# Row means of a 512 MiB array: loop loads moved from SyncE's hardware queue to GpSimd's software queue, eight runs as one packet

## The chip, the cores and the metric

The kernel runs on one core of a Trainium2 chip. The metric is the device time of one execution in microseconds (us); lower is better. The core has five engines that work side by side: TensorE (PE), VectorE (DVE), ScalarE (ACT), GpSimd (POOL) and SyncE (SP). They order their work by semaphores. Data moves between the chip's memory (HBM) and the on-chip buffers (SBUF, 128 partitions) through 16 DMA engines, which all issuing engines share.

## The reference

```python
def setup_inputs():
    return {
        "x": np.random.randn(64, 256, 8192).astype(np.float32),
    }

def reference(x: np.ndarray) -> np.ndarray:
    return np.mean(x, axis=2)
```

The input has 64 x 256 = 16384 rows of 8192 float32 numbers, 536.87 MB. The output is the mean of each row, 16384 numbers.

## The kernel before

**Tiling.** Each of the 128 partitions owns 127 consecutive rows. They are taken two at a time: 63 loads (NB) of two rows each, 64 KB for a partition, 8 MiB in all; the text calls them load 0 to load 62. The 127th owned row comes alone ("one", 4 MiB). The last 128 rows of the array are split into quarters, one quarter row for a partition, and come as four groups of 1 MiB, the last of them cut into four pieces, so that little work is left once the last bytes land.

**Buffers.** There are three SBUF buffers of 64 KB for a partition (NBUF = 3). Load g goes into buffer g mod 3. "one" and the groups use buffer 0 again at the end.

**SyncE issues every load** (lines 109 to 131). First come load 0 in two parts (L114 with a quarter of one row, L115 with the rest), load 1 and load 2 (L117). Then a loop of 20 rounds (L118) issues loads 3 to 62: for each of the three buffers it waits until the buffer's free semaphore is at least 1, takes 1 off it (L120), and issues the load (L121), whose address hangs on the loop's counter. Behind the loop SyncE waits for free semaphore 0 again and issues "one" (L125), three groups (L127) and four pieces (L129). At the end it stores the results (L133, L135).

**VectorE adds up.** It goes through the loads in order. A loop of 20 rounds (L160) waits for a buffer's arrival semaphore, which counts 16 for a load, takes the 16 off (L162), and reduces the buffer's two rows to two sums (L163); the end of the reduction adds 1 to the buffer's free semaphore. Loads 60 and 61 are reduced at L173. Load 62, "one", the groups and one piece go through `halves` (L145), one instruction that adds the two halves of its operand and sums up the result; one piece has a reduction of its own (L196).

**The others.** GpSimd prepares a small selection matrix (L81 to L93), waits for the owned rows' sums and multiplies them by 1/8192 (L104); their store leaves at L133. ScalarE sums two pieces (L209). TensorE adds the four quarters of the last rows (L218), and VectorE and ScalarE copy that to the row which is stored at L135.

**Order around the change.** All loads go through one hardware queue in the order of issue. A load of the loop can't be issued before the reduction that frees its buffer has ended. Each DMA engine moves the share of eight partitions, so eight runs of 64 KB of a full load.

The loop of the issuing engine:

```python
with eng.Fori(0, ROUNDS) as i:
    for b in range(NBUF):
        eng.wait_ge(free_sems[b], 1).then_inc(free_sems[b], -1)
        eng.dma_start(bufs[b][:], later[b][:, bass.ds(i, 1), :]).then_inc(
            in_sems[b], 16
        )
```

Of the kernel before, what the change touches and what calls it, by code (L numbers as in the profile page):

```python
# [6 lines left out]
ADD = mybir.AluOpType.add  # L7
X = mybir.AxisListType.X
# [3 lines left out]
def bass_global_avg_pool_1d_kernel(  # L12
# [6 lines left out]
    B, C, L = x.shape  # L19
# [4 lines left out]
    NB = OWN // 2  # L24
    NBUF = 3
    ROUNDS = NB // NBUF - 1
# [12 lines left out]
    owned = flat[0 : P * OWN, :].rearrange("(p r) l -> p (r l)", p=P)  # L39
# [4 lines left out]
    with ExitStack() as ctx:  # L44
        sb = lambda n, s: ctx.enter_context(nc.sbuf_tensor(n, s, F32))
        sem = lambda n: ctx.enter_context(nc.semaphore(n))
        res = sb("res", [P, OWN])
# [5 lines left out]
        bufs = [sb(f"buf{i}", [P, 2 * L]) for i in range(NBUF)]  # L53
# [3 lines left out]

        in_sems = [sem(f"in_sem{i}") for i in range(NBUF)]
        free_sems = [sem(f"free_sem{i}") for i in range(NBUF)]
        first_sem = sem("first_sem")  # L60
        one_sem = sem("one_sem")
        group_sems = [sem(f"group_sem{j}") for j in range(PER - 1)]
        piece_sems = [sem(f"piece_sem{c}") for c in range(NP)]
        owned_sem = sem("owned_sem")
# [9 lines left out]

        one = bufs[0][:, 0:L]
        group = lambda j: bufs[0][:, L + j * W : L + (j + 1) * W]

        eng = nc.gpsimd  # L80
# [18 lines left out]
            pattern=[[PER, G]],  # L99
            channel_multiplier=-1,  # L100
        ).then_inc(sel_sem, 1)
        eng.wait_ge(free_sems[0], 1)
        eng.wait_ge(owned_sem, 4)
        eng.tensor_scalar(  # L104
            scaled[:], res[:], inv, None, op0=mybir.AluOpType.mult
# [2 lines left out]

        eng = nc.sync
        pair = lambda g: owned[:, 2 * g * L : 2 * (g + 1) * L]  # L110
        later = owned[:, 2 * NBUF * L : 2 * NB * L].rearrange(
            "p (i b w) -> b p i w", i=ROUNDS, b=NBUF
        )
        eng.dma_start(bufs[0][:, 0:FIRST], owned[:, 0:FIRST]).then_inc(first_sem, 16)  # L114
        eng.dma_start(bufs[0][:, FIRST:], owned[:, FIRST : 2 * L]).then_inc(in_sems[0], 16)  # L115
        for b in range(1, NBUF):
            eng.dma_start(bufs[b][:], pair(b)).then_inc(in_sems[b], 16)  # L117
        with eng.Fori(0, ROUNDS) as i:  # L118
            for b in range(NBUF):
                eng.wait_ge(free_sems[b], 1).then_inc(free_sems[b], -1)  # L120
                eng.dma_start(bufs[b][:], later[b][:, bass.ds(i, 1), :]).then_inc(  # L121
                    in_sems[b], 16
                )
        eng.wait_ge(free_sems[0], 1)
        eng.dma_start(one, owned[:, 2 * NB * L :]).then_inc(one_sem, 16)  # L125
        for j in range(PER - 1):
            eng.dma_start(group(j), groups[j]).then_inc(group_sems[j], 16)  # L127
# [13 lines left out]
        eng = nc.vector  # L141

        def halves(ap, to, done):
            n = ap.shape[1] // 2
            eng.tensor_tensor_reduce(  # L145
                ap[:, 0:n],
                ap[:, 0:n],
                ap[:, n : 2 * n],
                scale=1.0,
                scalar=0.0,  # L150
                op0=ADD,
                op1=ADD,
                accum_out=to,
            ).then_inc(done, 1)

        eng.wait_ge(first_sem, 16)
        early = res[:, 0 : 2 * ROUNDS * NBUF].rearrange(
            "p (i b j) -> p i b j", i=ROUNDS, b=NBUF
        )
        with eng.Fori(0, ROUNDS) as i:  # L160
            for b in range(NBUF):
                eng.wait_ge(in_sems[b], 16).then_inc(in_sems[b], -16)  # L162
                eng.tensor_reduce(  # L163
                    early[:, bass.ds(i, 1), b, :],
                    bufs[b][:].rearrange("p (j l) -> p j l", j=2),
                    X,
                    ADD,
                ).then_inc(free_sems[b], 1)
        for b in range(NBUF):
            g = NB - NBUF + b  # L170
            eng.wait_ge(in_sems[b], 16)
            if b < 2:
                eng.tensor_reduce(  # L173
                    res[:, 2 * g : 2 * g + 2],
                    bufs[b][:].rearrange("p (j l) -> p j l", j=2),
                    X,
                    ADD,
                ).then_inc(free_sems[0] if b == 0 else owned_sem, 1)
            else:
                for j in range(2):  # L180
                    halves(
                        bufs[b][:, j * L : (j + 1) * L],
                        res[:, 2 * g + j : 2 * g + j + 1],
                        owned_sem,
                    )
# [17 lines left out]
        eng = nc.scalar  # L203
        for n, c in enumerate((0, 2)):
# [3 lines left out]
            to = PER - 1 + c  # L208
# [5 lines left out]
        eng = nc.tensor  # L214
# [45 lines left out]
```

## Time and profile before

| | |
|---|---|
| median of the 3 runs shown | 1243.48 us (1243.43 to 1244.08) |
| profiled execution | 1243.53 us |
| span of its instructions | 1242.3 us |
| VectorE busy | 1085.5 us in 78 instructions |
| HBM read | 536.87 MB, 432 GB/s over the span |
| transfers of the loop (L121) | 60, SyncE busy 333 ns with each issue |
| `halves` on 4096 + 4096 numbers (L145) | 3, mean 4424 ns |

The profile is of one execution. Its span runs from the first to the last instruction of the core; the execution's own time is 1.2 us longer. In a line of a group, the first part names the source line, the engine, the operation and the tiles with their shapes; behind the bar stand the busy time in total, the mean of one in ns, and the time for which the engine was idle just before such instructions, with what ended it. A line of the timeline has the start, the duration, the engine, the line and what it does; in square brackets stands the idle time before. Lines with DMA_DIRECT2D are issues of transfers; the number behind the size, or the last one, is the median time from issue to landing. In the view of slices the span is cut into 40 equal parts of 31 us, and GB/s is what the 16 DMA engines moved in each.

### The profile page before, as it was taken

How to read it: one execution, taken by the hardware profiler on the slowest of the kernel's cores; microseconds unless marked ns; L12 is line 12 of the kernel's file. 1: busy time of each engine (PE TensorE's matmuls, PEld its weight loads, DVE VectorE, ACT ScalarE, POOL GpSimd, SP SyncE). 2: the span in 40 equal slices, each digit the busy share in tenths (PEclk: the TensorE clock that was granted, in tenths of full speed). 3: DMA queues.
4: the chain of work that ended last, by engine and by line, in shares of the span. 5: the costliest groups of instructions: out<-in, count | busy, mean ns of one | idle time of the engine just before them, and what ended most of it. 6: DMA issues, size and time to landing. Idle time of an engine off the chain costs nothing. (4 is left out here: it accounts for less than half of the span.)

```text
span 1242.3 us, 636 instructions
## 1 busy us (share of the span) xinstructions
PE 1.7 (0%) x14; PEld 0.6 (0%) x14; DVE 1085.5 (87%) x78; ACT 3.0 (0%) x6; POOL 2.1 (0%) x8
## 2 busy tenths in 40 slices
PE   0000000000000000000000000000000000000000
PEld 0000000000000000000000000000000000000000
DVE  2898988989889898898898988989889898898988
ACT  0000000000000000000000000000000000000000
POOL 0000000000000000000000000000000000000000
DMA  9999999999999999999999999999999999999998
GB/s 405 439 439 439 439 433 411 439 439 439 439 439 422 422 439 439 439 439 439 433 411 439 439 439 439 439 437 407 439 439 439 439 439 437 409 437 439 439 439 374
DMA packets 10514, 536.94 MB, mean 432 GB/s; under 512 B 1297, under 2 KB 1554, under 8 KB 1810
## 3 DMA queue, kind: packets, MB, share of 16 engines
q1 hardware_dynamic: 10514, 536.94, 99.8%
HBM read 536.87 MB, written 0.07 MB: 432 GB/s over the span
## 5 line engine op out<-in xcount | busy, mean ns | idle before, releaser
L163 DVE TENSOR_REDUCE res<-buf 128x16384 f32 x60 | 1033.2, 17220 | 146.8 <-DVEq L162 146.8
L173 DVE TENSOR_REDUCE res<-buf 128x2 f32<-128x16384 f32 x2 | 34.4, 17220 | 4.0 <-DMA buf<-in_x_dram 4.0
L145 DVE CUSTOM_DVE_ANT_0 buf<-buf 128x4096 f32<-128x4096 f32 (+2 forms) x7 | 17.3, 2497 | 4.1 <-DMA buf<-in_x_dram 4.1
L209 ACT ACTIVATE buf<-buf 128x896 f32<-128x896 f32 (+1 forms) x2 | 1.4, 711 | 1236.7 <-DMA buf<-in_x_dram 1236.6
L104 POOL TENSOR_SCALAR scaled<-res 128x127 f32<-128x127 f32 x1 | 1.4, 1362 | 1233.3 <-DVE res L145 1233.3
L218 PE MATMUL psum<-sel,part 128*1 128x32 f32 x14 | 1.7, 225 | 1239.2 <-DVE part L145 1238.3
L209 ACT ACT_TABLE_LOAD x1 | 1.3, 1283 | 0.8 <-PEq L245 0.8
L218 PEld LDWEIGHTS psum<-sel,part 128*1 128x1 f32 x14 | 0.6, 81 | 1240.1 <-issue 1235.9
L196 DVE TENSOR_REDUCE part<-buf 128x1 f32<-128x256 f32 x1 | 0.4, 420 | 0.4 <-DMA buf<-in_x_dram 0.4
L200 DVE COPY row<-psum 1x32 f32<-1x32 f32 x1 | 0.2, 179 | 0.4 <-PE psum L218 0.4
L209 ACT ACTIVATION_READ_ACCUMULATOR buf<-buf 128x1 f32 x2 | 0.4, 188 | 0.0
L145 DVE DVE_READ_ACCUMULATOR2_ANT part<- 128x1 f32 x4 | 0.3, 82 | 0.0
L145 DVE DVE_READ_ACCUMULATOR2_ANT res<- 128x1 f32 x3 | 0.2, 83 | 0.0
L211 ACT ACTIVATE row<-psum 1x96 f32<-1x96 f32 x1 | 0.2, 223 | 0.0
L93 POOL TENSOR_SCALAR_AFFINE_SELECT sel<-sel 128x32 f32<-128x32 f32 x1 | 0.2, 215 | 0.1
L83 POOL TENSOR_SCALAR_AFFINE_SELECT sel<-sel 128x32 f32<-128x32 f32 x1 | 0.2, 213 | 0.1
L81 POOL MEMSET sel<- 128x32 f32 x1 | 0.1, 125 | 0.3 <-POOLq L245 0.3
L245 POOL MEMSET const-uint8-127<- 128x1 uint8 x1 | 0.1, 103 | 0.0
L245 POOL MEMSET const-bfloat16-1.0<- 128x1 bf16 x1 | 0.1, 102 | 0.0
L245 POOL MEMSET const-float32-0.0<- 128x1 f32 x1 | 0.1, 99 | 0.3 <-issue 0.3
L245 POOL MEMSET const-float32-1.0<- 128x1 f32 x1 | 0.1, 99 | 0.0
## 6 DMA issues: line engine op xcount, KB each, us to landing
buf<-in_x_dram SPq DMA_DIRECT2D x1, 7168.0 KB, 21.1
buf<-in_x_dram SPq DMA_DIRECT2D x4, 1024.0 KB, 34.1
buf<-in_x_dram SPq DMA_DIRECT2D x1, 4096.0 KB, 31.1
buf<-in_x_dram SPq DMA_DIRECT2D x62, 40.3
buf<-in_x_dram SPq DMA_DIRECT2D x1, 448.0 KB, 37.7
buf<-in_x_dram SPq DMA_DIRECT2D x1, 288.0 KB, 37.9
buf<-in_x_dram SPq DMA_DIRECT2D x1, 160.0 KB, 37.9
buf<-in_x_dram SPq DMA_DIRECT2D x1, 128.0 KB, 37.8
```

Of the source, the lines that this page charges most:

```text
L83: eng.affine_select(out=sel[:], in_=sel[:], compare_op=mybir.AluOpType.is_ge, fill=0.0, base=0, pattern=[[-PER, G]], channel_multiplier=1, ...
L93: eng.affine_select(out=sel[:], in_=sel[:], compare_op=mybir.AluOpType.is_ge, fill=0.0, base=PER - 1, pattern=[[PER, G]], channel_multipli ...
L104: eng.tensor_scalar(scaled[:], res[:], inv, None, op0=mybir.AluOpType.mult).then_inc(pool_sem, 1)
L145: eng.tensor_tensor_reduce(ap[:, 0:n], ap[:, 0:n], ap[:, n : 2 * n], scale=1.0, scalar=0.0, op0=ADD, op1=ADD, accum_out=to,).then_inc(done, 1)
L163: eng.tensor_reduce(early[:, bass.ds(i, 1), b, :], bufs[b][:].rearrange("p (j l) -> p j l", j=2), X, ADD,).then_inc(free_sems[b], 1)
L173: eng.tensor_reduce(res[:, 2 * g : 2 * g + 2], bufs[b][:].rearrange("p (j l) -> p j l", j=2), X, ADD,).then_inc(free_sems[0] if b == 0 els ...
L196: eng.tensor_reduce(part[:, PER + 2 : PER + 3], group(PER - 1)[:, a:z], X, ADD).then_inc(part_d, 1)
L200: eng.tensor_copy(row[:, P - G : P], psum[1][:, 0:G]).then_inc(row_sem, 1)
L209: eng.activation(ap, ap, COPY, accum_out=part[:, to : to + 1]).then_inc(part_a, 1)
L211: eng.activation(row[:, 0 : P - G], psum[0][:, 0 : P - G], COPY).then_inc(row_sem, 1)
L218: return eng.matmul(dst, part[:, n : n + 1], sel[:], start=start, stop=stop)
L245: nc = _bacc.Bacc("TRN2", target_bir_lowering=False, num_devices=1)
```

## The change

Loads 0 to 2 and the last loads ("one", groups, pieces) stay with SyncE. Loads 3 to 62 are issued by GpSimd, whose transfers go through a queue of its own with descriptors made by software. The loop has the same 20 rounds of three and the same wait for the free semaphore. Each transfer carries `single_packet=True`: the eight runs of a DMA engine are to make one packet.

The loads of the loop count on semaphores of their own (`soft_sems`), which are no longer counted down: VectorE waits for 16 more in each round, with a value that a register holds. The first three reductions stand ahead of VectorE's loop, which has 19 rounds now. The end of the reduction of load 60 is told by a new semaphore (`last_sem`), for which both SyncE (ahead of "one") and GpSimd (ahead of its scaling, now L116) wait. The shapes and the number of reductions are the same.

```diff
+        soft_sems = [sem(f"soft_sem{i}") for i in range(NBUF)]
+        last_sem = sem("last_sem")
...
         eng = nc.gpsimd
...
-        eng.wait_ge(free_sems[0], 1)
+        later = owned[:, 2 * NBUF * L : 2 * NB * L].rearrange(
+            "p (i b w) -> b p i w", i=ROUNDS, b=NBUF
+        )
+        with eng.Fori(0, ROUNDS) as i:
+            for b in range(NBUF):
+                eng.wait_ge(free_sems[b], 1).then_inc(free_sems[b], -1)
+                eng.dma_start(
+                    bufs[b][:], later[b][:, bass.ds(i, 1), :], single_packet=True
+                ).then_inc(soft_sems[b], 16)
+        eng.wait_ge(last_sem, 1)
         eng.wait_ge(owned_sem, 4)
...
         eng = nc.sync
...
-        with eng.Fori(0, ROUNDS) as i:
-            for b in range(NBUF):
-                eng.wait_ge(free_sems[b], 1).then_inc(free_sems[b], -1)
-                eng.dma_start(bufs[b][:], later[b][:, bass.ds(i, 1), :]).then_inc(
-                    in_sems[b], 16
-                )
-        eng.wait_ge(free_sems[0], 1)
+        eng.wait_ge(last_sem, 1)
         eng.dma_start(one, owned[:, 2 * NB * L :]).then_inc(one_sem, 16)
...
         eng = nc.vector
...
+        def sums(to, b):
+            return eng.tensor_reduce(
+                to, bufs[b][:].rearrange("p (j l) -> p j l", j=2), X, ADD
+            )
+
+        for b in range(NBUF):
+            eng.wait_ge(in_sems[b], 16)
+            sums(res[:, 2 * b : 2 * b + 2], b).then_inc(free_sems[b], 1)
...
-        with eng.Fori(0, ROUNDS) as i:
+        with eng.Fori(0, ROUNDS - 1) as i:
             for b in range(NBUF):
-                eng.wait_ge(in_sems[b], 16).then_inc(in_sems[b], -16)
...
+                eng.wait_ge(soft_sems[b], i * 16 + 16)
+                sums(early[:, bass.ds(i, 1), b, :], b).then_inc(free_sems[b], 1)
         for b in range(NBUF):
             g = NB - NBUF + b
-            eng.wait_ge(in_sems[b], 16)
+            eng.wait_ge(soft_sems[b], 16 * ROUNDS)
             if b < 2:
...
+                sums(res[:, 2 * g : 2 * g + 2], b).then_inc(last_sem if b == 0 else owned_sem, 1)
```

More of the change, by code (lines that the diff above doesn't have):

```diff
@@ L110, in bass_global_avg_pool_1d_kernel @@
         pair = lambda g: owned[:, 2 * g * L : 2 * (g + 1) * L]
-        later = owned[:, 2 * NBUF * L : 2 * NB * L].rearrange(
-            "p (i b w) -> b p i w", i=ROUNDS, b=NBUF
-        )
         eng.dma_start(bufs[0][:, 0:FIRST], owned[:, 0:FIRST]).then_inc(first_sem, 16)
@@ L117, in bass_global_avg_pool_1d_kernel @@
             eng.dma_start(bufs[b][:], pair(b)).then_inc(in_sems[b], 16)
-        with eng.Fori(0, ROUNDS) as i:
-            for b in range(NBUF):
-                eng.wait_ge(free_sems[b], 1).then_inc(free_sems[b], -1)
-                eng.dma_start(bufs[b][:], later[b][:, bass.ds(i, 1), :]).then_inc(
-                    in_sems[b], 16
-                )
-        eng.wait_ge(free_sems[0], 1)
+        eng.wait_ge(last_sem, 1)
         eng.dma_start(one, owned[:, 2 * NB * L :]).then_inc(one_sem, 16)
@@ L156, in bass_global_avg_pool_1d_kernel @@
         eng.wait_ge(first_sem, 16)
-        early = res[:, 0 : 2 * ROUNDS * NBUF].rearrange(
-            "p (i b j) -> p i b j", i=ROUNDS, b=NBUF
+        def sums(to, b):
[5 more added lines that the diff above has]
+            sums(res[:, 2 * b : 2 * b + 2], b).then_inc(free_sems[b], 1)
+        early = res[:, 2 * NBUF : 2 * ROUNDS * NBUF].rearrange(
+            "p (i b j) -> p i b j", i=ROUNDS - 1, b=NBUF
         )
-        with eng.Fori(0, ROUNDS) as i:
+        with eng.Fori(0, ROUNDS - 1) as i:
             for b in range(NBUF):
[L162 to L168, printed above, removed]
+                eng.wait_ge(soft_sems[b], i * 16 + 16)
+                sums(early[:, bass.ds(i, 1), b, :], b).then_inc(free_sems[b], 1)
         for b in range(NBUF):
             g = NB - NBUF + b
-            eng.wait_ge(in_sems[b], 16)
+            eng.wait_ge(soft_sems[b], 16 * ROUNDS)
             if b < 2:
[L173 to L178, printed above, removed]
+                sums(res[:, 2 * g : 2 * g + 2], b).then_inc(last_sem if b == 0 else owned_sem, 1)
             else:
```

## The prediction

> **What bounds the kernel now.** I read the page from the top: first busy shares and the rate by slices, then the DMA queues, then the costliest groups.
>
> ```profile
> span 1242.3 us, 636 instructions
> ...
> PE 1.7 (0%) x14; PEld 0.6 (0%) x14; DVE 1085.5 (87%) x78; ACT 3.0 (0%) x6; POOL 2.1 (0%) x8
> ...
> GB/s 405 439 439 439 439 433 411 439 439 439 439 439 422 422 439 439 439 439 439 433 411 439 439 439 439 439 437 407 439 439 439 439 439 437 409 437 439 439 439 374
> DMA packets 10514, 536.94 MB, mean 432 GB/s; under 512 B 1297, under 2 KB 1554, under 8 KB 1810
> ...
> q1 hardware_dynamic: 10514, 536.94, 99.8%
> ...
> L163 DVE TENSOR_REDUCE res<-buf 128x16384 f32 x60 | 1033.2, 17220 | 146.8 <-DVEq L162 146.8
> ...
> buf<-in_x_dram SPq DMA_DIRECT2D x1, 7168.0 KB, 21.1
> ...
> buf<-in_x_dram SPq DMA_DIRECT2D x62, 40.3
> ```
>
> The reader is to see one hardware queue whose packets fill 99.8% of the 16 DMA engines' span, and a VectorE (DVE) that is busy for 87% and idle before each reduction. The kernel is bound by the transfers. Call the 63 two-row loads load 0 to load 62. The timeline gives their pace, and what stands in the queue when the first loop load is issued:
>
> ```profile
> 22.65 17.22 DVE L163 TENSOR_REDUCE res<-buf 128x16384 f32 x1 [22.65 <-DVEq L162]
> 40.15 19.62 SPq L121 DMA_DIRECT2D buf<-in_x_dram  x2
> 41.98 17.22 DVE L163 TENSOR_REDUCE res<-buf 128x16384 f32 x1 [2.11 <-DVEq L162]
> 61.34 17.22 DVE L163 TENSOR_REDUCE res<-buf 128x16384 f32 x1 [2.14 <-DVEq L162]
> ```
>
> Reductions start 19.33 us apart and take 17.22, so DVE waits about 2.1 us for each load. From the first start (22.65) to the sixtieth (1162.78) it is 1140.13 / 59 = 19.324 us a load: 8.389 MB in that time is 434 GB/s, the rate that the table by stretches gives from 100 to 1180 us too. The first loop load, load 3, is issued at 40.15, 0.28 us after reduction 0 ended (22.65 + 17.22 = 39.87). Load 1 then still lacks its last microseconds, and load 2 waits whole. So load 3 lands only 40.3 us later, in its turn. The end of the timeline matters too:
>
> ```profile
> 1201.18 17.22 DVE L173 TENSOR_REDUCE res<-buf 128x2 f32<-128x16384 f32 x1 [2.10 <-DMA buf<-in_x_dram]
> 1220.54 4.42 DVE L145 CUSTOM_DVE_ANT_0 buf<-buf 128x4096 f32<-128x4096 f32 x1 [2.15 <-DMA buf<-in_x_dram]
> ...
> 1230.22 4.43 DVE L145 CUSTOM_DVE_ANT_0 buf<-buf 128x4096 f32<-128x4096 f32 x1 [0.90 <-DMA buf<-in_x_dram]
> ```
>
> Load 62 is taken up at 1220.54 and the 4 MiB load behind it ("one", L125) at 1230.22, each after DVE had waited.
>
> **The change, part by part.** The sum is made against the profiled execution, 1243.53 us (span 1242.3 and 1.2 around it), 0.05 above the median of 1243.48.
>
> *Issuing.* SyncE loses 60 issues of 0.33 us with some 0.07 of register work; they lay beside transfers and give back nothing. GpSimd (POOL) gets 60 issues. It has no DMA issue in this trace, so the price is bounded: from no dearer than SyncE's 0.4 us upwards. The cover is what is queued ahead. At an issue the load in front is still to be moved, so the engines need the new load some 21 us later (40.3 - 19.33). Up to that a slow issue costs nothing in the steady stretch; beyond it every microsecond costs one for each of 60 loads. I take 0. Behind POOL's loop stands only the scaling (L104, L116 after), which before starts at 1234.84, long after the last loop issue at 1180.2. DVE's register work before a reduction was 57 ns and remains about that, inside the 2.1 us of waiting.
>
> *Packets.* An engine's share of a load, eight runs of 64 KB, becomes one packet instead of eight. A row gives a price: "one" has runs of 32 KB, and its 4 MiB took 1230.22 - 1220.54 = 9.68 us, where half a full load takes 9.662. Four more runs on each engine thus cost 0.018 us, 4.5 ns each (2 to 7 with the rounding of the two starts). If that price belongs to the packet and not to the run, seven fewer save 0.032 us a load, 1.9 us over 60 loads (0.8 to 2.9); if to the run, 0. I take 1.9. The Trainium skill, page "DMA: Bandwidth & Descriptors", "Why small descriptors are slow (HBM only)", puts about 3 cycles on each packet; the 4.5 ns agree in size, and by its 850 MHz the sum would hold 1.5 us (an estimate) instead of 1.9.
>
> *The change-over.* This is the large term. In the kernel before, load 3 cannot overtake load 2: one queue. Now load 2 is in the hardware queue, load 3 in another queue of the same 16 engines, issued while load 2 waits. No row shows two queues at once, so bounds: nothing, if load 2 goes first or both advance evenly; and the following, if an engine alternates by packets, one 64 KB run of load 2 against all eight runs of load 3. Then load 3 goes nearly whole ahead of load 2. At 59.2 reduction 1 ends (41.98 + 17.22) and load 4 is issued, before load 3 is through (some 64), so load 4 overtakes too. Load 2 is complete only when all three are, at about 42 + 3 x 19.33 = 100 us. DVE must have load 2 first; until then loads 3 and 4 sit in their buffers unread, and no buffer is free. So load 5 waits for the reduction of load 2, and the engines stand idle. Price: 0.23 us from landing to start (40.15 + 40.3 = 80.45, the reduction of load 3 starts at 80.68), the reduction 17.22, 0.28 to the issue, and a load into an empty queue instead of a queued one. For this the start of the kernel has a row: L114 and L115 are issued from 0.80 on, and the second lands 21.1 us after its issue at 1.27, at 22.4; 21.6 us in all against a pace of 19.33, 2.3 us more. Sum 0.23 + 17.22 + 0.28 + 2.3 = 20.0 us. Then DVE has loads 3 and 4 to reduce (to 151.6) and gains 2.1 us a load on the transfers. Load 6 is issued at 134.7, while load 5 moves until 139, and later issues have more room, so the hole comes once. I take this end, because the diff itself makes the turns unequal, eight to one. The Trainium skill, same page, "Queues, rings and completion order", says that an engine goes round its queues at packet granularity; by it the term is 20.0, and with even turns 0; no run so far shows it.
>
> *The tail.* SyncE's last loads are issued, as before, when load 60 is reduced (1199.1), but now from another queue than load 62. With whole-packet turns they take one run of 32 KB (9.68 / 8 = 1.2 us) ahead of load 62. DVE then starts its halves 1.2 us late and is 0.3 late at "one" (it had 0.90 of waiting there); the remaining loads' waits, 0.55 before a later group, swallow that. I take 0; at most 0.3.
>
> Sum: 1243.53 + 0 - 1.9 + 20.0 + 0 = 1261.6, forecast as **1262 us**; its own range is 1260 to 1266 (packet price kept: 1263.5; POOL's first byte up to 2 us later than SyncE's).
>
> **The rivals.**
>
> *No hole* (the other side). Load 2 keeps its place or gets at least half of each engine. With even shares it lands at about 80 beside load 3, the reduction of load 2 runs to 98, and load 4, issued at 59.2, keeps the engines busy to 100: load 5 comes in time. Against the hole, then, it takes only that load 2 gets four runs or more in the time of one software load. For it: the bytes and the buffers are the same, and DVE has 2.1 us a load to make good 19 us of delay. Time: 1243.5 - 1.9 to 1243.5, so 1241.6 to 1243.5.
>
> *The eight runs are not one turn.* Software and hardware queue alternate run by run. The head costs nothing (even shares), but in the tail load 62 shares with the 32 KB runs of "one" and lands 8 x 1.2 = 9.7 us late, 1230.2. Its two halves (8.7), "one" (4.35), three groups (3.7), and the last pieces and the copy (1.3) follow without a wait and end near 1248.3, where the copy started at 1240.95: +7.3, **1251 us**.
>
> *The software queue is slower in steady run.* Each load leaves a gap, from 0.04 us (then 2.4 us in all decide) to the whole 2.3 us of a load into an empty queue, 60 x 2.3 = +138. Against it: two loads are outstanding at nearly all times. Most likely a few tenths: 1255 to 1300, with or without the hole.
>
> *More gain than priced* (no hole, and the hand-over from load to load shortened too): 60 x 0.05 = 3 us, 1240.5. The Trainium skill's same page, "Specifications", sets a ceiling of 435 GB/s, which no run here passes: 2.9 us by estimate.
>
> **How the numbers follow.** Hole 0.46; no hole 0.26; run by run 0.12; slower queue 0.12; more gain 0.04. A measurement of this kernel tells about 0.2% (2.5 us) from no change. Below 1241.0: the last case and a rest of the second, 0.06. Within 1241.0 to 1246.0: no hole, 0.25. Slower: 0.69. The range 1241 to 1266 holds the second and third case and nearly all of the first, 0.8; the slower queue is left out.
>
> **What would show it.** Right: the third reduction starts near 100 us instead of 61.34; loads 3 and 4 have landed before it; the rate by slices has one dip of about 20 us' worth in the stretch from 100 to 120; five to seven reductions then follow without idle time; after that starts are 19.29 apart, not 19.324. Wrong: third reduction at 61.3 or near 80 and no dip (no hole); load 62's halves near 1230 (run by run); a pace above 19.35 in the later stretch (slower queue), which would also show GpSimd's issue spans longer than the cover; a pace of 19.324 refutes the packet term alone.

## The result and the profile after

The changed kernel takes 1250.48 us (1250.39 to 1250.51, 4 runs) against 1243.75 before (4 runs, the three of the table of before and a fourth): ratio 1.0055, 95% interval 1.0043 to 1.0068. It is slower by 6.7 us. The forecast was 1262 with a range of 1241 to 1266: the sign and the range hold, the size does not: 18.5 us slower were forecast, 6.7 were measured.

From the page of the changed kernel, the lines that answer to those of before:

```profile
span 1249.4 us, 573 instructions
...
GB/s 403 436 436 436 436 436 436 436 436 436 426 422 428 436 436 436 436 436 436 436 436 436 436 436 436 432 424 420 436 436 436 436 436 436 436 436 436 436 420 287
...
q0 software_dynamic: 8640, 503.32, 93.0%
q1 hardware_dynamic: 1874, 33.62, 6.3%
...
L162 DVE TENSOR_REDUCE res<-buf 128x16384 f32 (+1 forms) x62 | 1067.0, 17219 | 151.5 <-DMA buf<-in_x_dram 151.5
L111 POOL DMA_DIRECT2D buf<-in_x_dram x60 | 31.8, 530 | 1147.8 <-POOLq L110 1147.8
...
buf<-in_x_dram POOLq DMA_DIRECT2D x60, 39.9
```

The 60 loads stand in a software queue now. There is no hole of 20 us: the slices from 93 to 125 us (the fourth) still move 436 GB/s. The low slice is the last one, 287 against 374 before. (436 instead of 439 in the full slices is no slower pace: a slice is 31.23 us wide instead of 31.06, and the count in it is one of whole runs.) A load of the queue is recorded with 8640 / 60 = 144 packets, 128 runs and 16 completions (four-byte writes, one from each engine, by which its share is reported as landed), just as before.

The timeline of the changed kernel at the change-over:

```profile
40.52 0.71 POOL L111 DMA_DIRECT2D buf<-in_x_dram  x1 [38.91 <-POOLq L110]
41.71 17.22 DVE L162 TENSOR_REDUCE res<-buf 128x2 f32<-128x16384 f32 x1 [2.04 <-DMA buf<-in_x_dram]
59.67 0.53 POOL L111 DMA_DIRECT2D buf<-in_x_dram  x1 [18.45 <-POOLq L110]
78.00 137.10 DVE L162 TENSOR_REDUCE res<-buf 128x2 f32<-128x16384 f32 x8 [19.07 <-DMA buf<-in_x_dram]
```

Load 2 is taken up at 78.00 instead of 61.34, and then eight reductions follow without a pause: DVE's reserve of 2.1 us a load makes the delay good. After that the pace is the old one, by two reductions after (L162) and the same two before (L163):

```profile
235.47 17.22 DVE L162 TENSOR_REDUCE res<-buf 128x16384 f32 x1 [2.10 <-DMA buf<-in_x_dram]
1162.77 17.22 DVE L162 TENSOR_REDUCE res<-buf 128x16384 f32 x1 [2.10 <-DMA buf<-in_x_dram]
235.35 17.22 DVE L163 TENSOR_REDUCE res<-buf 128x16384 f32 x1 [2.10 <-DVEq L162]
1162.78 17.22 DVE L163 TENSOR_REDUCE res<-buf 128x16384 f32 x1 [2.09 <-DVEq L162]
```

Between them are 48 loads, 19.319 us each after and 19.321 before. At 235 us the changed kernel is 0.1 us behind (its first reduction started 0.2 us earlier), at 1163 us no longer. The end, with the last copy of before as the last line:

```profile
1199.19 0.33 SPq L128 DMA_DIRECT2D buf<-in_x_dram  x1
...
1201.25 17.22 DVE L162 TENSOR_REDUCE res<-buf 128x2 f32<-128x16384 f32 x1 [2.09 <-DMA buf<-in_x_dram]
1230.30 4.43 DVE L148 CUSTOM_DVE_ANT_0 buf<-buf 128x4096 f32<-128x4096 f32 x1 [11.83 <-DMA buf<-in_x_dram]
...
1248.01 0.18 DVE L202 COPY row<-psum 1x32 f32<-1x32 f32 x1 [0.36 <-PE psum L220]
...
1240.95 0.18 DVE L200 COPY row<-psum 1x32 f32<-1x32 f32 x1 [0.36 <-PE psum L218]
```

The reduction of load 61 starts at 1201.25, 0.07 later than before. Load 62 is taken up at 1230.30 instead of 1220.54, and the last copy starts at 1248.01 instead of 1240.95: 7.06 us, and all but 0.07 of it arises between these lines. Why load 62 is late, the records of the DMA engines in the trace show. Each row below is one turn of all 16 engines, with the start of its first run:

```
us from the span's start, bytes of a run, queue
1200.57  65536 software (load 62, first run)
1202.99  32768 hardware ("one")
1204.20  65536 software
1206.61  32768 hardware
1207.82  65536 software
```

The engines alternate between the two queues run by run, and go on so until all eight runs of "one" are through. The same stands at the change-over: from 46 us a run of load 3 and a run of load 2 take turns, 64 KB each, until load 2's last run starts at 72.6. The completion takes a turn too: on the 16 engines load 2's four-byte completion write stands at 77.4 and later, behind one more 64 KB run of the software queue, so that load 2, complete in its data at 75.3, is taken up at 78.0.

### The profile page after: what moved, and what is told of

It reads as the page before. It is cut to its first block, busy times and chain, and to the rows that moved or that the text cites. A ratio compares the mean times of both kernels' runs of the same rounds, so it can differ in the third digit from the quotient of the medians.

```text
span 1249.4 us, 573 instructions
## 1 busy us (share of the span) xinstructions
PE 1.5 (0%) x14; PEld 0.7 (0%) x14; DVE 1084.5 (87%) x78; ACT 3.1 (0%) x6; POOL 33.9 (3%) x68
## 3 DMA queue, kind: packets, MB, share of 16 engines
q0 software_dynamic: 8640, 503.32, 93.0%
## 5 line engine op out<-in xcount | busy, mean ns | idle before, releaser
L162 DVE TENSOR_REDUCE res<-buf 128x16384 f32 (+1 forms) x62 | 1067.0, 17219 | 151.5 <-DMA buf<-in_x_dram 151.5
L111 POOL DMA_DIRECT2D buf<-in_x_dram x60 | 31.8, 530 | 1147.8 <-POOLq L110 1147.8
L116 POOL TENSOR_SCALAR scaled<-res 128x127 f32<-128x127 f32 x1 | 1.4, 1364 | 62.4 <-DVE res L148 62.4
```

Source lines behind the costliest of these rows:

```text
L111: eng.dma_start(bufs[b][:], later[b][:, bass.ds(i, 1), :], single_packet=True).then_inc(soft_sems[b], 16)
L116: eng.tensor_scalar(scaled[:], res[:], inv, None, op0=mybir.AluOpType.mult).then_inc(pool_sem, 1)
L162: return eng.tensor_reduce(to, bufs[b][:].rearrange("p (j l) -> p j l", j=2), X, ADD)
```

## The experiments

**Theory.** Two queues on the same engines take turns, one run each, whatever the size of the run (8 to 64 KB in these experiments), the kind of queue and the flag. The whole loss is load 62 sharing its engines with the loads behind it. **Rivals:** the flag does something; the software queue itself is slow; the late load 2 costs something. The edits are cut to the lines that matter; remarks behind # are added.

### Without the flag

```diff
-                    bufs[b][:], later[b][:, bass.ds(i, 1), :], single_packet=True
+                    bufs[b][:], later[b][:, bass.ds(i, 1), :]
```

> The changed kernel without the one-packet flag. Theory (the two queues take turns run by run, and the flag changes nothing): 1250.5 us, pace 19.32 us a load, load 62 taken up at about 1230. Rival (the flag saves some of the packet price of 1.9 us, or lengthens the software queue's turns): time apart from 1250.5 by 0.8 to 2.9 us, or load 62 taken up later than 1231.

Measured: 1250.93 us (1250.43 to 1251.26). Load 62 is taken up at 1231.02, a hair beyond the 1231 that was to speak for the flag, but the whole profiled execution lags by 0.7 from 236 us on, and from load 61 it is 29.01 us, against 29.05 with the flag; the turns are the same. The median is 0.45 us higher, within the 0.8 us over which these runs scatter. So a small difference isn't excluded here; a longer turn of the flagged queue is.

### All behind load 62 in the same queue

```diff
-        eng.wait_ge(last_sem, 1)                                  # on SyncE
-        eng.dma_start(one, owned[:, 2 * NB * L :]).then_inc(one_sem, 16)
...
         eng.wait_ge(last_sem, 1)                                  # on GpSimd, behind its loop
+        eng.dma_start(one, owned[:, 2 * NB * L :]).then_inc(one_sem, 16)
...
```

> The loads behind load 62 go through the software queue too, issued by GpSimd behind its loop; the head is shared as in the changed kernel. Theory (all of the loss is load 62 sharing the engines with the loads behind it): 1250.5 - 7.1 = 1243.4 us, at most 0.7 more for GpSimd's issues; load 62 taken up at 1220.6. Rival (the software queue or the late load 2 costs the time): stays above 1248.

Measured: 1244.04 us (1243.75 to 1244.73), ratio to before 1.0003, interval 0.9994 to 1.0013. The loss is gone. Its timeline has the end of before again, load 61 to load 62 in 19.36 us:

```profile
1202.60 17.22 DVE L161 TENSOR_REDUCE res<-buf 128x2 f32<-128x16384 f32 x1 [2.10 <-DMA buf<-in_x_dram]
1221.96 4.43 DVE L147 CUSTOM_DVE_ANT_0 buf<-buf 128x4096 f32<-128x4096 f32 x1 [2.14 <-DMA buf<-in_x_dram]
```

### The loads behind load 62 wait until it has landed

```diff
         eng.wait_ge(last_sem, 1)
+        eng.wait_ge(soft_sems[2], 16 * ROUNDS)
         eng.dma_start(one, owned[:, 2 * NB * L :]).then_inc(one_sem, 16)
```

> SyncE issues the loads behind load 62 only when load 62 has landed. Theory: no sharing, but the engines run empty once: 1243.5 + 2.3 (a load into an empty queue) = 1245.8 us, load 62 taken up at 1220.6. Rival (the hardware queue is slow beside the software one whatever the sharing): stays at 1250 or above.

Measured: 1247.08 us (1246.8 to 1247.94). Right in kind: the time falls between the two, and load 62 is taken up 19.31 us after load 61. The time is 1.3 above what was expected:

```profile
1221.21 4.42 DVE L149 CUSTOM_DVE_ANT_0 buf<-buf 128x4096 f32<-128x4096 f32 x1 [2.09 <-DMA buf<-in_x_dram]
1221.27 0.33 SPq L129 DMA_DIRECT2D buf<-in_x_dram  x1
...
1233.49 4.43 DVE L149 CUSTOM_DVE_ANT_0 buf<-buf 128x4096 f32<-128x4096 f32 x1 [3.50 <-DMA buf<-in_x_dram]
```

"one" is taken up 12.28 us after load 62 instead of 9.68, 2.6 later. From load 62's start to the last copy it is 23.64 instead of 20.41 us, 3.2 more, where 2.3 had been taken as the price of an empty queue. The rest of the 1.3 lies ahead of load 61, whose reduction starts at 1201.90 instead of 1201.18.

### Two hardware queues

The kernel before, with the loads behind load 62 issued by ScalarE (and `last_sem` as the signal).

```diff
-        eng.wait_ge(free_sems[0], 1)                              # on SyncE
-        eng.dma_start(one, owned[:, 2 * NB * L :]).then_inc(one_sem, 16)
...
+        eng = nc.scalar
+        eng.wait_ge(last_sem, 1)
+        eng.dma_start(one, owned[:, 2 * NB * L :]).then_inc(one_sem, 16)
...
```

> The kernel before, every loop load on SyncE, but the loads behind load 62 are issued by ScalarE through its own hardware queue. Theory (two queues on the same engines, of whatever kind, take turns run by run): load 62 taken up at about 1230, before + 7 = 1250.6 us. Rival (the loss belongs to the software queue): 1243.5 to 1244.

Measured: 1250.55 us (1250.42 to 1250.59), ratio 1.0056, interval 1.0042 to 1.007. The loss needs no software queue:

```profile
1201.05 17.22 DVE L166 TENSOR_REDUCE res<-buf 128x2 f32<-128x16384 f32 x1 [2.09 <-DMA buf<-in_x_dram]
...
1230.11 4.43 DVE L138 CUSTOM_DVE_ANT_0 buf<-buf 128x4096 f32<-128x4096 f32 x1 [11.84 <-DMA buf<-in_x_dram]
```

### Everything in the software queue

Beside the end, loads 0 to 2 too are issued by GpSimd, ahead of everything else that it does.

```diff
-        eng.dma_start(bufs[0][:, 0:FIRST], owned[:, 0:FIRST]).then_inc(first_sem, 16)   # on SyncE
...
+        eng.dma_start(bufs[0][:, 0:FIRST], owned[:, 0:FIRST]).then_inc(first_sem, 16)   # on GpSimd
...
```

> All loads go through the software queue, issued by GpSimd. Theory: one queue, no turns at either end: load 2 taken up near 61.5, load 62 near 1220.6, 1243.4 us plus a first byte later by 0 to 1 us. Rival (late load 2 had a cost hidden in the changed kernel): below the run with only the tail moved by more than 1 us.

Measured: 1244.3 us (1244.08 to 1244.62), ratio 1.0006, interval 0.9997 to 1.0015. The first reduction starts at 23.71, 0.9 to 1.2 later than in the runs with SyncE's first loads (22.5 to 22.9), and the time is 0.3 above the run with only the end moved. So the shared start costs something, about a microsecond at most. Counted from the first reduction to the one near 236 us: 212.70 before, 212.76 here, 213.01 in the changed kernel, and 213.42, 213.94 and 213.33 in the three runs above that share the start and nothing else new there. That is 0.3 to 1.2 us. The records of the DMA engines show what most of it hangs on. Load 5 is issued at 95.9 to 96.3, only some 3 us before load 4 is through. In the three runs some engines start load 5 late and stay behind: the 16 engines start their runs within 0.4 to 0.6 us of one another in load 4, and within 0.9 to 1.6 at 150 us. A load has landed only when the last engine is through. The spread grows by 0.7, 1.0 and 0.5 us (without the flag, with the end moved, with the wait), and the three lose 0.7, 1.2 and 0.6. In the changed kernel's profile no engine is late there (a spread of 0.3 to 0.4 us throughout); what makes its own 0.3 us the runs leave open.

### Load 2 in small runs: 8 to 1, 4 to 1, 2 to 1

These three test the prediction's hole, by making the turns of load 2 and load 3 as unequal as it supposed. The edit for 8 to 1 (VectorE waits for a count of 128 for load 2); the others have 4 and 2 in place of 8, and counts of 64 and 32:

```diff
-        for b in range(1, NBUF):
-            eng.dma_start(bufs[b][:], pair(b)).then_inc(in_sems[b], 16)
+        eng.dma_start(bufs[1][:], pair(1)).then_inc(in_sems[1], 16)
+        S = 2 * L // 8
+        for c in range(8):
+            eng.dma_start(
+                bufs[2][:, c * S : (c + 1) * S], pair(2)[:, c * S : (c + 1) * S]
+            ).then_inc(in_sems[2], 16)
```

> The changed kernel, but SyncE brings load 2 in eight transfers with runs of 8 KB, so that a turn of load 2 is an eighth of a turn of load 3. Theory (turns by run, not by bytes): load 2 is overtaken by loads 3 and 4, is taken up near 100 us, the engines run empty once, and the hole of 20 us of the prediction appears: 1250.5 + 20 = 1270 us (1268 to 1273). Rival (turns by bytes or time): load 2 is taken up near 80 and the time stays at 1250.5 to 1251.

> The same with four transfers of 16 KB runs. Theory: load 2 still has some 8 of 32 runs left when load 4 is through, is taken up near 100, and the hole is as long as with turns of 8 to 1: 1271 to 1272 us. Rival (the hole grows evenly with the ratio): about 1266.

> The changed kernel with load 2 in two transfers of 32 KB runs, so that its turns are half of load 3's. Theory: load 2 has all its bytes when load 4 is half through, near 89; it is reduced from 90 to 107, the first bytes of load 5 come 2 us later at 109, and the engines have run empty since 99: a hole of 10 us, 1250.5 + 10 = 1260.5 us (1258 to 1262). Rival (a hole comes only when load 2 is quite overtaken): 1250.5.

Measured: 1271.75 us (1271.67 to 1271.94) with 8 to 1, 1271.63 (1271.5 to 1271.79) with 4 to 1, 1266.82 (1266.63 to 1266.96) with 2 to 1. With 8 to 1 the hole stands where the prediction had it. Its timeline, and the stretch from 100 to 120 us of its table by stretches, in which the DMA engines are busy for 0.09 and move 29 GB/s (the last two columns):

```profile
60.03 0.53 POOL L111 DMA_DIRECT2D buf<-in_x_dram  x1 [18.43 <-POOLq L110]
100.37 68.60 DVE L166 TENSOR_REDUCE res<-buf 128x2 f32<-128x16384 f32 x4 [41.08 <-DMA buf<-in_x_dram]
118.31 0.53 POOL L111 DMA_DIRECT2D buf<-in_x_dram  x1 [57.76 <-POOLq L110]
```

```profile
100.00:120.00 20.00, 0.00 (x0) 0.00 (x0) 19.63 (x2) 0.00 (x0) 0.53 (x1) 1.00 0.09 29
```

It costs 1271.75 - 1250.48 = 21.3 us, where 20.0 had been worked out. The hole is full with 4 to 1 already. Load 2's reduction with 4 to 1 and with 2 to 1:

```profile
100.08 68.60 DVE L166 TENSOR_REDUCE res<-buf 128x2 f32<-128x16384 f32 x4 [40.84 <-DMA buf<-in_x_dram]
95.28 68.60 DVE L166 TENSOR_REDUCE res<-buf 128x2 f32<-128x16384 f32 x4 [35.99 <-DMA buf<-in_x_dram]
```

With 2 to 1 the expectation was 6 us too low. It let load 2 have the same time before load 3 comes as in the changed kernel (two runs of 64 KB, 4.85 us), but by the records load 3's first run came after three runs of 32 KB on nine engines and after four on the other seven. So a further turn was missing, and the completion's turn came on top: load 2's data were through by 92.5, its completions stood at 94.4 to 94.9, and it was taken up at 95.28, not at 90.

### Small runs in the loop, with and without the flag

```diff
-                eng.dma_start(
-                    bufs[b][:], later[b][:, bass.ds(i, 1), :], single_packet=True
-                ).then_inc(soft_sems[b], 16)
+                S = 2 * L // 8
+                for c in range(8):
+                    eng.dma_start(
+                        bufs[b][:, c * S : (c + 1) * S],
+                        later[b][:, bass.ds(i, 1), c * S : (c + 1) * S],
+                        single_packet=True,
+                    ).then_inc(soft_sems[b], 16)
```

(DVE waits for 128 more in each round; the second kernel has False.)

> The changed kernel with each loop load cut in eight transfers of 8 KB runs, each flagged as one packet. Theory (flag without effect, price of 4.5 ns on each run): pace 19.32 + 56 x 0.0045 = 19.58 us, 60 x 0.25 = 15 us, and load 62 in 64 small turns lets nearly all loads behind it past, some 17 us in place of 7: about 1275 us, the same as without the flag. Rival (a flagged transfer of 64 KB for an engine is one turn and one packet): pace 19.32 to 19.36 and load 62 only 9.7 us late, 1250 to 1253.

> As the run before, without the flag. Theory: about 1275 us, within 0.5 of the flagged one. Rival: 10 to 25 us above the flagged one.

Measured: 1278.68 us (1278.55 to 1278.75) with the flag, 1278.8 (1278.64 to 1278.85) without. The flag changes nothing with runs of 8 KB either: no longer turn, no lower price (in both, load 62 is taken up 39.0 us after load 61, and by the records with the flag its 8 KB runs take turns with the 32 KB runs of "one"). The pace from the reduction at 140.33 to the one at 1180.36 (with the flag) is 1040.03 / 53 = 19.623 us, 0.304 above 19.319: with 56 more runs and seven more completions on each engine, 5.4 ns for each further run, or 4.8 if the completions cost as much. Both expected times were 3.7 us too low, most of it by the pace: 60 loads at 0.304 are 18.2 us, where 15 had been expected.

## Why the prediction was wrong

- **The change-over: the step that failed.** The prediction took its upper end, "because the diff itself makes the turns unequal, eight to one". The turns were equal, one 64 KB run each, and the term was 0.3 us in the changed kernel's profile (up to 1.2 in the others with this start) instead of 20.0. The mechanism behind the number held: where turns were made unequal by the size of load 2's runs, the hole came, in its place and with 21.3 us. What was read wrongly was the unit of a turn. The Trainium skill, "DMA: Bandwidth & Descriptors", "Queues, rings and completion order", has engines go round at packet granularity, with 9 to 17 descriptors a typical packet. The runs agree only if a packet is a single run here, with or without the flag.
- **The condition for no hole was too mild as well.** The prediction let "four runs or more in the time of one software load" be enough for load 2. With 2 to 1, load 2 gets one 32 KB run for each 64 KB run, eight in the turns of a software load and so the bytes of four 64 KB runs, and that kernel lost 16.3 us (1266.82 - 1250.48). With equal turns it gets eight full runs, which the even shares of the same paragraph rightly had as harmless.
- **The tail: mis-sized with it.** Taken as 0, at most 0.3; it was 7.0 of the 7.1 us. Whole-packet turns would have let load 62 through; run by run it shares with all eight runs of "one". The prediction's third case, "the eight runs are not one turn", had this sum: load 62 at 1230.2 and +7.3 us, 1251, with a chance of 0.12. Measured: 1230.30, +7.0, 1250.5. It also had the head right: even shares leave the DMA engines busy, though only just, as load 5 shows. That the sign and the stated range held is luck as far as the chosen mechanism goes, whose own range was 1260 to 1266: the kernel is slower by a term that was taken at 0, and the wide range held it because it took in this rival.
- **Packets: 0 instead of 1.9 us.** The pace stayed (19.319 against 19.321, so 0.1 us over 60 loads). The price belongs to the run, flagged or not: the runs of 8 KB cost the same with and without the flag. Whether the flag is dropped somewhere or honoured without effect on turns and price, no run tells.
- **Issuing: right.** A software issue takes GpSimd 0.53 us (the first 0.71), and the 60 of them lie within the 21 us of cover. The "up to 2 us" for a later first byte from GpSimd were an upper bound from no row; with every load on GpSimd the first reduction started 0.9 to 1.2 us later, and 0.5 of that is the later first issue (1.41 instead of 0.92).

The choice was made from a label in the diff; no row of the profile spoke for longer turns, and the profile of before, where a load counts as 128 runs and 16 completions, could not show what the label does. Between ends so far apart, the case in which the label does nothing deserved the larger chance.

## What to carry to other kernels

Loads that must land in order belong in one queue; a second queue on the same DMA engines, software or hardware, lets later loads in by turns of one run each (seen with runs of 8 to 64 KB). Early on such a delay costs little if the consumer has a reserve and the engines stay busy (0.3 to 1.2 us here); at the end, what the last big load loses to its successors is lost, less the waits behind it (9.8 us late, 7.1 lost). When queues must share, set the size of the runs: the load in the larger runs gets the larger share.

## What the runs showed that was not expected

- The turn does not depend on a run's size: 64 KB against 8 KB gave the 64 KB queue eight ninths of the engine while both had runs (2.42 against 0.31 us a turn), and load 2 came 39 us late (100.37 against 61.34).
- A load's completion takes a turn of its own, here 2.4 us behind the last data (load 2: data through on the last engine at 75.3, completions from 77.4 to 77.7, taken up at 78.0).
- The software queue keeps the pace of the hardware queue when loads stand queued: 19.319 us for 8 MiB, 434 GB/s.
- An emptied queue cost 3.2 us at the end (the run in which the last loads wait), 0.9 more than the 2.3 taken from the start of the kernel.
